# Linear attention on one core: each head pair's output stored by two DMAs of 1 MB in place of one of 2 MB

## The chip, the cores and the metric

The kernel runs on 1 core of a Trainium2 chip. The metric is device microseconds; three runs of the kernel before gave 126.98, 126.93 and 126.97, a median of 126.97.

## What is computed

Linear attention for 8 × 12 heads, 512 positions and 64 features, FP32 in and out:

```python
Q_feat = np.maximum(0, Q) + 1
K_feat = np.maximum(0, K) + 1
KV = np.einsum('bhkd,bhkv->bhdv', K_feat, V)
K_sum = np.sum(K_feat, axis=2)
numerator = np.einsum('bhqd,bhdv->bhqv', Q_feat, KV)
denominator = np.einsum('bhqd,bhd->bhq', Q_feat, K_sum)
return (numerator / (denominator[:, :, :, None] + 1e-10)).astype(np.float32)
```

Three inputs of 12.58 MB are read and one output of 12.58 MB is written.

## The kernel before

The 96 heads are worked on in six steps, numbered s = 0 to 5. The code calls a step a pair: it holds two blocks (n = 0, 1) of eight heads, each block being 128 partitions of 32 rows. So one pair has 1 MB of each input in BF16 (2 MB in FP32) and 2 MB of FP32 output.

All loads but the first half of K go through POOL's DMA queue, which also turns FP32 into BF16 on the way (`load`, line 128). ACT and DVE copy V into a block-diagonal form (L156), DVE makes the features of K and Q (L144, L164), PE sums K features times V (L175), transposes the Q features (L199) and multiplies them by the sums (L216). DVE then takes the reciprocal of the denominators (L232) and multiplies (L233) into the output tile `o_sb`, in eight parts a pair. These are `norms(s, part)`; in the written orders they are called n40 for pair 4, part 0, and so on.

`o_sb` has 128 partitions, eight entries and 2 KB in each entry: 16 KB in a partition. In the output each entry is a block of 256 KB in which every partition owns 2 KB. Part p = 4e + 2i + u writes the entries e + 2u and e + 2u + 4, one half (i) of each: parts 0 to 3 fill the even entries and parts 4 to 7 the odd ones. There are four `o_sb` buffers (`OUT_BUFS`). The first K load borrows one of them at the start, so pair 4 is the first to write into a buffer that has held an output: that of pair 0.

`store(s, ms, engine)` (L135) writes the entries `ms` of pair s. `stores_of(s)` says into how many stores a pair is cut and which parts each needs. Pairs 0 to 3 have one store of all eight entries (2 MB); pair 4 has two, of the even and of the odd entries (1 MB each); pair 5 has one of 1 MB and two of 512 KB. A store is called s20 for pair 2, store 0. Pair 5's are issued by SP on its own queue, the others by POOL.

Each engine's order is written out by hand in `ORDER`, and `trace_all` issues each engine's instructions in exactly that order. POOL's is all loads and then all stores:

```python
POOL="""
    lv2 lk2 lq2 lv3 lq3 lk3 lk4 lv4 lq4 lv5 lk5 lq5 s00 s10 s20 s30 s40 s41
""",
SP="""
    s50 s51 s52
""",
```

(the loads of pairs 0 and 1 come before these). The waits between engines are made from the tiles that instructions read and write.

Of the kernel before, what the change touches and what calls it, by code (L numbers as in the profile page):

```python
# [40 lines left out]
        e40 v500 c43 e41 v511 v512 c42 c50 e50 c51 e51 c53 c52  # L41
    """,
    POOL="""
        lv2 lk2 lq2 lv3 lq3 lk3 lk4 lv4 lq4 lv5 lk5 lq5 s00 s10 s20 s30 s40 s41
    """,
    SP="""
        s50 s51 s52
# [5 lines left out]
def kernel(  # L53
# [210 lines left out]
    last = NPAIR - 1  # L264
    done = set()

    def needs(engine, task):
# [36 lines left out]
        if x == "no":  # L304
            return [("om", s, at[0])] + [("st", s - OUT_BUFS, j) for j in stores_of(s - OUT_BUFS)]
        if x == "st":
            return [("no", s, p) for p in stores_of(s)[at[0]][1]]

    def stores_of(s):

        if s < 0:
            return {}
        if s < last - 1:
            return {0: (slice(0, 8), range(8))}
        halves = {e: (slice(e, 8, 2), range(4 * e, 4 * e + 4)) for e in range(2)}
        if s < last:
            return halves
        return {
            0: halves[0],
            1: (slice(1, 8, 4), (4, 6)),  # L320
            2: (slice(3, 8, 4), (5, 7)),
        }

    def trace(engine, task):
        x, s, *at = task
        if x == "load":
            load(at[0], s)
        elif x == "kf":
            k_features(s, at[0])
        elif x == "vb":  # L330
            copy = nc.vector.tensor_copy if engine == "DVE" else nc.scalar.copy
            v_block(s, at[0], at[1], copy)
        elif x == "qf":
            q_features(s)
        elif x == "kv":
            keys_values(s, *at)
        elif x == "ev":
            weights(s, at[0])
        elif x == "tr":
            transposes(s, at[0])  # L340
        elif x == "tc":
            transposed(s, at[0], nc.vector.tensor_copy if engine == "DVE" else nc.scalar.copy)
        elif x == "om":
            out_matmuls(s, at[0])
        elif x == "no":
            norms(s, at[0])
        elif x == "st":
            store(s, stores_of(s)[at[0]][0], nc.sync if s == last else nc.gpsimd)
# [70 lines left out]
```

## Time and profile before

| | |
|---|---|
| median of 3 runs | 126.97 us |
| profiled execution | 126.98 us |
| its span, first to last instruction | 125.2 us |
| mean granted TensorE clock | 0.924 |
| busy share PE / DVE / ACT / POOL | 65% / 75% / 59% / 18% |
| POOL's DMA queue | 28.84 MB, 94.1% of the DMA engines' span |
| SP's DMA queue | 3.15 MB, 6.8% |
| HBM | 37.75 MB read, 12.58 MB written |
| stores of 2 MB from POOL | 4, median 23.9 us from issue to landing |
| stores of 1 MB from POOL | 2, median 13.5 us |

The span is the time between the first and the last instruction of the profiled execution; what is around it makes up the rest of the 126.98. Lines are marked L and the number in the listing. A DMA has 16 completions, one for each DMA engine, and has landed when its semaphore has all of them; the time from issue to landing holds the time that it waits behind other DMAs of its queue.

### The profile page before, as it was taken

To read this page: it belongs to the slowest core of one execution; us is meant where nothing else is said; L and a number is where in the kernel's file an instruction comes from. 1 tells how busy PE (TensorE), PEld (TensorE's weight loads), DVE (VectorE), ACT (ScalarE), POOL (GpSimd) and SP (SyncE) were. 2 spreads that over 40 slices of the span, in tenths; PEclk is the share of its full clock that TensorE was granted. 3 is DMA by queue.
4 is the path that set the end of the run, shared out by engine and by line. 5 is a ranking of instruction groups with operands and counts; after the bars stand their busy time and mean duration, and the time that the engine had idled before them with its cause. 6 is when DMAs were issued, how large, how long until landed. Compare 5 with 4: busy or idle time off the path is not lost.

```text
span 125.2 us, 2347 instructions
## 1 busy us (share of the span) xinstructions
PE 81.9 (65%) x960; PEld 61.6 (49%) x960; DVE 93.8 (75%) x188; ACT 74.3 (59%) x94; POOL 22.6 (18%) x48
## 2 busy tenths in 40 slices
PE   0000099974989896699439999969997889650000
PEld 0000067853667775477327767656875567430000
DVE  4799962469489796995789799999999796993000
ACT  7538000674856999849990399989999357400000
POOL 6991042000006000060000580002002010200000
PEclk9999999999599999999995999999999999995555
DMA  3999999999999999999999999999999999999992
GB/s 89 339 211 212 217 211 217 211 216 215 215 213 215 222 207 213 215 217 215 215 212 213 221 212 212 212 217 213 216 395 411 417 414 391 390 383 390 386 384 88
DMA packets 8666, 32.12 MB, mean 257 GB/s; under 512 B 464, under 2 KB 464, under 8 KB 8528
## 3 DMA queue, kind: packets, MB, share of 16 engines
q0 software_dynamic: 7440, 28.84, 94.1%
q1 hardware_dynamic: 1216, 3.15, 6.8%
q8 instruction: 7, 0.11, 0.3%
q14 instruction: 3, 0.02, 0.0%
HBM read 37.75 MB, written 12.58 MB: 402 GB/s over the span
## 4 chain that ended last, share of the span: by engine, by line
DMA 54%; DVE 13%; ACT 8%; issue 7%; PE 5%; POOL 3%; POOLq 0%; DVEq 0%
DMA q_raw<-in_Q_dram 34%; DMA out_dram<-o_sb 20%; DVE o_sb L233 7%; ACT v_all L156 5%; DVE qf L164 4%; ACT qt L204 2%; PE kva_ps L175 2%; PE o_ps L216 2%; PE qt_ps L199 1%; DVE recip L232 1%; ACT kva L189 1%; POOL v_raw L128 1%; DVE kf L144 1%; POOL k_raw L128 1%; DVE v_all L156 0%
## 5 line engine op out<-in xcount | busy, mean ns | idle before, releaser
L175 PE MATMUL kva_ps<-v_all,kf 128*128 128x260 bf16 x384 | 54.0, 293 | 21.7 <-DVE v_all L156 17.6
L175 PEld LDWEIGHTS <-kf 128*128 128x128 bf16 x384 | 37.1, 103 | 31.7 <-DVE v_all L156 18.0
L156 ACT COPY v_all<-v_raw 32x2048 bf16<-32x2048 bf16 x19 | 36.0, 1896 | 4.8 <-DVE v_all L258 3.2
L233 DVE TENSOR_TENSOR o_sb<-o_ps,recip 128x512 f32<-128x512 f32 x48 | 33.2, 692 | 2.2 <-DMA out_dram<-o_sb 0.6
L204 ACT COPY qt<-qt_ps 128x1024 bf16<-128x1024 bf16 x24 | 23.8, 1014 | 10.6 <-PE qt_ps L199 10.4
L216 PE MATMUL o_ps<-kva,qt 128*64 128x130 bf16 x384 | 20.3, 229 | 7.8 <-DVE o_sb L233 5.4
L144 DVE TENSOR_SCALAR kf<-k_raw,shift,least 128x2048 bf16<-128x2048 bf16 x22 | 17.1, 819 | 6.9 <-PE kva_ps L175 5.0
L156 DVE COPY v_all<-v_raw 32x2048 bf16<-32x2048 bf16 x29 | 20.2, 697 | 0.8
L216 PEld LDWEIGHTS <-qt 128*64 128x64 bf16 x384 | 12.7, 111 | 16.4 <-DVE o_sb L233 6.8
L189 ACT CAST kva<-kva_ps 64x256 bf16<-64x256 f32 x24 | 8.9, 372 | 17.9 <-PE kva_ps L175 17.5
L199 PE MATMUL qt_ps<-identity,qf 128*128 128x128 bf16 x192 | 14.9, 222 | 1.4 <-DVE qf L164 1.0
L199 PEld LDWEIGHTS <-qf 128*128 128x128 bf16 x192 | 12.1, 99 | 2.9 <-DVE qf L164 1.1
L164 DVE TENSOR_SCALAR qf<-q_raw 128x1024 bf16<-128x1024 bf16 x24 | 8.8, 432 | 5.2 <-DMA q_raw<-in_Q_dram 5.2
L128 POOL DMA_DIRECT2D v_raw<-in_V_dram x7 | 4.8, 687 | 41.0 <-DVE recip L232 18.0
L232 DVE RECIPROCAL recip<-o_ps 128x8 f32<-128x8 f32 x48 | 9.6, 201 | 2.6 <-PE o_ps L216 2.3
L135 POOL DMA_DIRECT2D out_dram<-o_sb x6 | 5.5, 913 | 30.1 <-DVE recip L232 20.6
L128 POOL DMA_DIRECT2D k_raw<-in_K_dram x6 | 4.2, 696 | 12.8 <-DVE kf L144 12.8
L128 POOL DMA_DIRECT2D q_raw<-in_Q_dram x6 | 5.0, 840 | 1.2 <-DVE qf L164 1.2
L258 DVE MEMSET v_all<- 128x2600 f32 x2 | 4.5, 2225 | 1.1 <-issue 1.1
L193 ACT CAST kva<-kva_ps 64x4 bf16<-64x4 f32 x24 | 4.1, 170 | 0.0
L259 ACT COPY v_all<-zero 128x1560 f32<-128x1560 f32 x2 | 2.9, 1488 | 0.0
L144 DVE TENSOR_SCALAR kf<-o_sb,shift,least 128x2048 bf16<-128x2048 f32 x2 | 2.6, 1340 | 0.0
(18 smaller groups left out, 6.6 us busy)
## 6 DMA issues: line engine op xcount, KB each, us to landing
out_dram<-o_sb POOLq DMA_DIRECT2D x4, 2048.0 KB, 23.9
q_raw<-in_Q_dram POOLq DMA_DIRECT2D x6, 1024.0 KB, 21.5
k_raw<-in_K_dram POOLq DMA_DIRECT2D x5, 1024.0 KB, 16.3
v_raw<-in_V_dram POOLq DMA_DIRECT2D x5, 1024.0 KB, 18.4
out_dram<-o_sb POOLq DMA_DIRECT2D x2, 1024.0 KB, 13.5
o_sb<-in_K_dram SPq DMA_DIRECT2D x1, 1024.0 KB, 4.9
v_raw<-in_V_dram POOLq DMA_DIRECT2D x2, 512.0 KB, 8.5
out_dram<-o_sb SPq DMA_DIRECT2D x1, 1024.0 KB, 10.6
```

The source lines that it names most:

```text
L128: nc.gpsimd.dma_start(out=t[:, ns[0] : ns[-1] + 1], in_=drams[x][:, 2 * s + ns[0] : 2 * s + ns[-1] + 1])
L135: engine.dma_start(out=o_dram[:, 8 * s : 8 * s + 8][:, ms], in_=outs[s][:, ms], single_packet=engine is nc.gpsimd,)
L144: nc.vector.tensor_scalar(out=kf[:, :, a], in0=raw["k", s, n], scalar1=shift[:, a : a + 1], scalar2=least[:, a : a + 1], op0=ALU.add, op1= ...
L156: copy(out=v_alls[n][ps, :, b * D : b * D + D], in_=raw["v", s, n][ps])
L164: nc.vector.tensor_scalar(out=qf[:, :, cs, n], in0=rows[:, :, cs], scalar1=1.0, scalar2=1.0, op0=ALU.add, op1=ALU.max,)
L175: nc.tensor.matmul(kva_pss[s, n], lhsT=kfs[s, n][:, c].rearrange("p a d -> p (a d)"), rhs=v_alls[n][:, c], start=(c == 0), stop=(c == ROWS ...
L189: nc.scalar.copy(out=kva[po, a::2, n, 0:D], in_=kva_ps[pi, 0 : 4 * D].rearrange("p (b d) -> p b d", b=4),)
L199: nc.tensor.transpose(qt_ps[:, c, r], qfs[s][:, r, 2 * i + c], identity)
L204: copy(out=qts[s][:, 2 * i : 2 * i + 2], in_=qt_pss.pop((s, i)).rearrange("p c r q -> p c q r"),)
L216: nc.tensor.matmul(o_ps[64 * t : 64 * t + 64, c // 2, (c % 2) * W : (c % 2) * W + W], lhsT=qts[s][:, 4 * i + c, 16 * k : 16 * k + 16], rhs ...
L232: nc.vector.reciprocal(out=recip, in_=cells[:, :, :, :, D:D1])
L233: nc.vector.tensor_tensor(out=outs[s][:, e + 2 * u :: 4, 4 * i : 4 * i + 4].rearrange("p n (b c) d -> p b c n d", b=2), in0=cells[:, :, :, ...
```

## The change

Pairs 0 to 3 are stored like pair 4: one DMA for the even entries, as soon as parts 0 to 3 are done, and one for the odd entries after parts 4 to 7. POOL's order names eight stores for these pairs instead of four. Pairs 4 and 5 are stored as before.

```diff
     POOL="""
-        lv2 lk2 lq2 lv3 lq3 lk3 lk4 lv4 lq4 lv5 lk5 lq5 s00 s10 s20 s30 s40 s41
+        lv2 lk2 lq2 lv3 lq3 lk3 lk4 lv4 lq4 lv5 lk5 lq5 s00 s01 s10 s11 s20 s21 s30 s31 s40 s41
     """,
...
         if s < 0:
             return {}
-        if s < last - 1:
-            return {0: (slice(0, 8), range(8))}
         halves = {e: (slice(e, 8, 2), range(4 * e, 4 * e + 4)) for e in range(2)}
         if s < last:
             return halves
```

## The prediction

> **What bounds the kernel now.** I read the 40 slices first, since the change touches only transfers.
>
> ```profile
> DMA  3999999999999999999999999999999999999992
> GB/s 89 339 211 212 217 211 217 211 216 215 215 213 215 222 207 213 215 217 215 215 212 213 221 212 212 212 217 213 216 395 411 417 414 391 390 383 390 386 384 88
> ```
>
> The 16 DMA engines are full from the second slice to the last but one. The 211 to 222 GB/s of slices 3 to 29 are loads that read FP32 and write BF16, so about 430 GB/s are read; from slice 30 (90.8 us) on there are only stores. No engine row is like this: the page's first part gives DVE, the busiest, 75%. Next I asked where the stores are issued, in the timeline of POOL:
>
> ```profile
> 71.78 0.72 POOL L128 DMA_DIRECT2D q_raw<-in_Q_dram  x1
> 72.50 2.15 POOL L135 DMA_DIRECT2D out_dram<-o_sb  x2
> 85.28 0.89 POOL L135 DMA_DIRECT2D out_dram<-o_sb  x1 [10.63 <-DVE recip L232]
> 95.73 0.91 POOL L135 DMA_DIRECT2D out_dram<-o_sb  x1 [9.56 <-DVE o_sb L233]
> 102.69 0.77 POOL L135 DMA_DIRECT2D out_dram<-o_sb  x1 [6.05 <-DVE recip L232]
> 107.34 0.75 POOL L135 DMA_DIRECT2D out_dram<-o_sb  x1 [3.89 <-DVE recip L232]
> ```
>
> These are, in order, the last load, s00 and s10 together, s20, s30, s40, s41. All stores stand in POOL's order behind all loads. In the trace's DMA records of POOL's queue the last of the 16 completions of each comes at: last load 91.95, s00 97.25, s10 102.30, s20 107.31, s30 113.22, s40 116.12, s41 120.07; then SP's s50 to s52, the last at 123.58. (The waiting engine sees it some 0.5 us later, s00 at 97.75 below.) The queue serves its DMAs in order and each waits for its turn: s20 is issued about 17 us before s10 has landed, s30 11 us before s20 has, s40 10 us before s30 has, s41 9 us before s40 has. So the store stage lasts as long as its bytes take, and not as long as anything that releases them. The last DVE instruction ends at 113.96, 9.6 us before the last landing.
>
> Third, whether anything waits for a store, in the chain of waits (start, length, what) and in DVE's waits:
>
> ```profile
> 72.50 25.25 DMA out_dram<-o_sb
> 97.75 0.03 issue
> 97.78 0.02 DVEq L233
> 97.80 0.04 issue
> 97.84 0.69 DVE o_sb L233
> ```
> ```profile
> DVE o_sb L233 <- DMA out_dram<-o_sb: 0.6, 1, 0.6
> ```
>
> One wait, 0.6 us: n40, the first division of pair 4, writes the o_sb buffer that s00 empties (four buffers, and the first K load has used one of them). The chain shows this as 25 us of DMA, but DVE only waits for the last 0.6 of it.
>
> Last, the store rate in stretches (length, engines, PE clock, DMA share, GB/s at the end):
>
> ```profile
> 92.00:95.00 3.00, 2.33 (x37) 1.66 (x34) 2.93 (x7) 2.94 (x6) 0.00 (x0) 1.00 1.03 423
> 97.00:101.00 4.00, 3.40 (x43) 2.64 (x41) 3.33 (x11) 1.15 (x2) 0.00 (x0) 1.00 1.02 417
> 103.00:107.00 4.00, 3.78 (x64) 2.96 (x64) 2.85 (x8) 3.09 (x8) 0.46 (x1) 1.00 1.03 394
> 107.00:111.00 4.00, 2.21 (x45) 1.36 (x42) 3.73 (x11) 1.01 (x1) 0.75 (x1) 1.00 1.01 385
> 112.50:114.50 2.00, 0.25 (x8) 0.09 (x4) 1.43 (x3) 0.00 (x0) 0.00 (x0) 0.60 1.01 391
> ```
>
> s00 and s10 move at 417 to 423 GB/s, s20 at about 394, s30 at 385, and s40, already a half of 1 MB, at 391. The rate falls while whole stores run, before the first half is in flight.
>
> **The change, part by part.** The sum is made against the profiled execution (126.98 us, span 125.2; 1.8 lie around the span); it is 0.01 above the median of 126.97.
>
> *Bytes and pieces.* Nothing changes: 12.58 MB written, runs of 2 KB at the output in both forms. All POOL store records, those of the halves s40 and s41 too, are 4 KB packets. Cost 0, if the rate stays (see the rivals).
>
> *Four more DMAs in POOL's queue.* Each ends with one completion record on each of the 16 engines. What a DMA costs between others, I take from the loads: 1 MB loads land every 4.895 us, the 512 KB loads at the start every 2.4575. Two small ones take 4.915, so one more DMA costs 0.020 us. For stores the completion record itself takes 9 ns against 22 for loads, which is the low end; the high end would be that half of s10 costs as much as s40, in the first rival. Four times 0.020 = 0.08 us, on the path, since the queue has no gap. I take it, as the loads are the only rows where just the size differs.
>
> The Trainium skill, "DMA: Bandwidth & Descriptors", section "Anatomy of one DMA — SWDGE (gpsimd) path", fits a DMA from GpSimd at about 2.0 us plus its bytes over 436 GB/s; its own account is that most of the 2.0 is waiting for completion. By that formula taken serially, four more DMAs would be an estimated 8 us, a time of 135.0.
>
> *POOL's issue time.* A 1 MB store takes 0.75 to 0.77 us, a 2 MB one 0.89 to 1.18, so s00, s01, s10, s11 take 4 × 0.76 = 3.0 instead of 2.15: 0.9 us more, once, at 72.5. Hidden by the queue's backlog: s00 has its turn only at about 90.6, 15 us after all four are issued. Nothing on POOL is behind them but stores, s20 being ready some microseconds later. Without the backlog it would cost the 0.9.
>
> *Stores issued earlier.* s20 and s30 now wait for four norms instead of eight and go out several microseconds earlier; s21 and s31 go out when the whole ones did. They come to a queue that is busy until 102 and 107, so that brings 0.
>
> *n40's wait.* It needs entries 0 and 4, both in the half with e = 0. If the wait is for that half alone, it ends about 2.5 us before 97.75, and DVE's 0.6 us disappear; if for both, it ends 0.02 to 0.04 later. What is late next is the stores of pairs 4 and 5, at most 0.6 earlier in queues with 9 us of backlog: 0 at the end. Bounds -0.6 to 0, taken 0, because the last landing is 9.6 us behind DVE.
>
> Sum: +0.08 us, 127.05 from the median. A difference of 0.2% is 0.25 us, about what a measurement of this kernel can tell from no change, so this counts as the same.
>
> **Rivals.**
>
> *Slower: halves are written at a lower rate.* A half takes every other entry: its pieces are 4 KB apart in o_sb and 512 KB apart in the output, where those of the whole lie side by side and 256 KB apart. The only half that runs almost alone, s40, lands 2.742 us after s30 (mean over the 16 engines); whole stores take 5.077, 5.015, 5.234 and 5.493. If a half costs 2.742 from the start, eight make 21.94 against 20.82: +1.12 us, 128.1. For it: s00 and s10 are the fastest stores and the only early ones, and no half is seen at 420 GB/s. Against it: s30, whole, is as slow as two times s40, so the fall looks tied to time or place, not to shape. It decides as soon as halves lose over a fifth of this (0.25 us). The early rate is the thing the change could spoil, and there is no row for it; so this stays a large case.
>
> *Faster: the late stores keep the early rate.* I do not know why s20 and s30 are slower than s10 with the same shape. If it is a state that the engines drift into (their completions of one DMA lie 1.4 us apart at the last load, 2.1 at s30), more and shorter DMAs in another order might delay it. At s10's 5.015 per 2 MB, s20 would gain 0.22, s30 0.48, and the 4 MB behind them 0.9: 125.4 with all of it, 126.65 with a quarter. No row shows a half helping.
>
> *Faster by the earlier wait.* The 0.6 us of n40 reach the end: 126.4. Against it are the 9.6 us of backlog. Small.
>
> *Each DMA pays its latency.* If the queue drained before each further DMA, four would cost several microseconds: the first V load of 512 KB lands 6.8 us after its issue by the page's row although its share of the queue is 2.46 us, so 4.3 each, 17 in all, 144. The DMA row of 9s and landings at 4.895 us intervals speak against it. The trace so also disagrees with the skill's formula as a serial cost.
>
> That the change doesn't do what it says I exclude: order and table agree on two stores for each pair up to 4.
>
> **How the numbers follow.** Same, +0.08: 0.43. Slower by the rate: 0.36, and 0.01 for latency. Faster: 0.15 by a kept rate, 0.05 by the wait. The likeliest is the sum, 127.05, whose own range is 126.9 to 127.3. The whole range goes up to the full price of the first rival, 128.1, and down to 126.4; the larger gains of a kept rate and the latency case are left out. Chances: 0.20, 0.43, 0.37.
>
> **What would show it.** Right: landings at mean intervals whose two halves sum to 5.0 to 5.1 in pairs 0 and 1, last completion within 0.25 us of 123.58, DVE's wait for out_dram gone, more POOL busy time and no new wait behind it. The slower rival: 2.7 us for each half from s00 on, and under 400 GB/s in slices 30 to 33. The faster: over 400 in slices 34 to 38. Wrong altogether: a gap in the DMA row, or POOL's later stores waiting for a landing.

## The result, and the profile after

The changed kernel takes 126.67 us (median of 14 runs) against 126.97 (14 runs): a ratio of 0.9974, with a 95% interval of 0.9967 to 0.9981. That is 0.30 us faster, where the prediction had it 0.08 slower, at 127.05 with 126.9 to 127.3 around it. The profiled execution took 126.69 us, its span 124.9.

The 40 slices of the changed kernel:

```profile
DMA  3999999999999999999999999999999999999993
GB/s 87 336 210 214 216 214 216 210 216 215 215 215 210 222 207 218 213 214 218 213 215 215 211 218 211 215 215 213 218 374 419 413 415 392 388 384 382 385 384 146
```

The DMA engines are as full as before, and the fall from between 413 and 419 GB/s to 392 and less is where it was. The same stretches as before (GB/s at the end of a line):

```profile
92.00:95.00 3.00, 3.00 (x39) 2.28 (x37) 2.90 (x6) 2.92 (x7) 0.00 (x0) 1.00 1.03 421
97.00:101.00 4.00, 4.00 (x51) 3.02 (x49) 3.92 (x10) 2.48 (x2) 0.75 (x1) 1.00 1.03 416
103.00:107.00 4.00, 3.78 (x57) 2.79 (x55) 2.85 (x8) 3.15 (x11) 0.75 (x1) 1.00 1.02 393
107.00:111.00 4.00, 2.55 (x48) 1.70 (x48) 3.73 (x10) 1.63 (x2) 0.75 (x1) 1.00 1.02 385
112.50:114.50 2.00, 0.97 (x14) 0.48 (x10) 1.93 (x5) 0.00 (x0) 0.00 (x0) 0.50 1.01 381
```

421, 416, 393, 385 against 423, 417, 394, 385: halves move as whole stores do at the same place. (In the last stretch both kernels write halves, at 381 and 391.) POOL's timeline:

```profile
71.88 0.72 POOL L128 DMA_DIRECT2D q_raw<-in_Q_dram  x1
72.59 3.15 POOL L135 DMA_DIRECT2D out_dram<-o_sb  x4
78.21 0.75 POOL L135 DMA_DIRECT2D out_dram<-o_sb  x1 [2.46 <-DVE recip L232]
86.61 0.75 POOL L135 DMA_DIRECT2D out_dram<-o_sb  x1 [7.65 <-DVE recip L232]
89.97 0.75 POOL L135 DMA_DIRECT2D out_dram<-o_sb  x1 [2.60 <-DVE o_sb L233]
97.15 0.75 POOL L135 DMA_DIRECT2D out_dram<-o_sb  x1 [6.43 <-DVE o_sb L233]
```

s20 and s30 go out 7 to 8 us ahead of s21 and s31, and the four stores of pairs 0 and 1 take 3.15 us of POOL. The output tensor's own view says who waits for a store:

```profile
who waited for it (us, times):
busy tenths in 40 slices 0000000000000000000000072202100202200000
```

Nobody is listed, where before DVE had its 0.6 us.

So far all is as predicted, and none of it makes the kernel faster. The last landing, as the engine that waits for it sees it, is at 124.01 us against 123.92 before: 0.09 us later. The span is nevertheless 0.31 shorter. The time went after the last landing: from there to the end of the span it is 1.28 us before and 0.88 after. These are POOL's last records in the trace (number in order of start, start, length in ns, instruction); of these the profile's page counts only s41 as busy. All but s41 belong to the line that closes the program (L414 in the listing):

```
before                                      changed
66  107.322 14171 DRAIN                     72  108.006 13308 DRAIN
67  107.343   754 DMA (s41)                 73  108.028   752 DMA (s41)
68  124.090    17 wait for all engines      74  124.179    17 wait for all engines
69  124.517    17 release all engines       75  124.261    17 release all engines
70  124.602   141 DRAIN                     76  124.342    88 DRAIN
71  124.772   118 clear semaphores          77  124.459   118 clear semaphores
```

Between the wait and the release of the other engines, POOL stands for 0.427 us before and for 0.082 after; the DRAIN that follows is 0.05 shorter too. Together these 0.40 us, less the 0.09 of the later landing, make the 0.31 of the span. The page has one more difference, in the part on queues. Before:

```profile
q8 instruction: 7, 0.11, 0.3%
q14 instruction: 3, 0.02, 0.0%
```

Changed:

```profile
q8 instruction: 7, 0.11, 0.3%
q14 instruction: 4, 0.03, 0.1%
```

Queue 14 fetches instructions, 8 KB at a time. Three of the records stand at like times in both kernels (43.1, 58.8 to 59.4, 111.8 to 112.6 us). The changed kernel has a fourth at 101.4. The kernel before has its fourth at 125.2, behind the end of its span, as the window from 123.9 to 126 us shows:

```profile
DMA  0000000000000000000000000400000000000000
...
q14 instruction: 1, 0.01, 1.1%
```

### The profile page after: what moved, and what is told of

The parts are those of the page before. It is cut to its first block, busy times and chain, and to the rows that moved or that the text cites. A ratio compares the mean times of both kernels' runs of the same rounds, so it can differ in the third digit from the quotient of the medians.

```text
span 124.9 us, 2353 instructions
## 1 busy us (share of the span) xinstructions
PE 82.9 (66%) x960; PEld 62.1 (50%) x960; DVE 93.8 (75%) x188; ACT 74.2 (59%) x94; POOL 24.8 (20%) x52
## 3 DMA queue, kind: packets, MB, share of 16 engines
q1 hardware_dynamic: 1216, 3.15, 6.9%
## 4 chain that ended last, share of the span: by engine, by line
DMA 39%; DVE 32%; PE 11%; POOL 6%; issue 3%; ACT 1%; POOLq 0%
DMA q_raw<-in_Q_dram 20%; DMA k_raw<-in_K_dram 18%; DVE o_sb L233 14%; PE kva_ps L175 7%; DVE kf L144 6%; DVE v_all L156 5%; DVE recip L232 3%; DVE qf L164 3%; PE o_ps L216 3%; POOL kva L380 2%; POOL v_raw L128 2%; PE qt_ps L199 1%; POOL q_raw L128 1%; POOL k_raw L128 1%; ACT qt L204 1%
## 5 line engine op out<-in xcount | busy, mean ns | idle before, releaser
L216 PE MATMUL o_ps<-kva,qt 128*64 128x130 bf16 x384 | 20.8, 233 | 6.9 <-DVE o_sb L233 4.8
L135 POOL DMA_DIRECT2D out_dram<-o_sb x10 | 7.7, 773 | 28.5 <-DVE recip L232 19.5
```

Source lines behind the costliest of these rows:

```text
L135: engine.dma_start(out=o_dram[:, 8 * s : 8 * s + 8][:, ms], in_=outs[s][:, ms], single_packet=engine is nc.gpsimd,)
L216: nc.tensor.matmul(o_ps[64 * t : 64 * t + 64, c // 2, (c % 2) * W : (c % 2) * W + W], lhsT=qts[s][:, 4 * i + c, 16 * k : 16 * k + 16], rhs ...
```

## The theories

**A**: POOL stands still for about 0.4 us at one place of its instruction stream, where a new block of instructions begins. Four more DMAs and the waits with them (80 POOL records in place of 74) push the end sequence past that place, so that the place falls where POOL waits for a norm anyway. The split itself costs about what the prediction said. **B**: the split helps through the transfers, and the end sequence is a coincidence. **C**: smaller stores are written at a lower rate.

## The experiments

**Whole stores, six more POOL instructions.**

```diff
+    spare = const.tile([P, 16], FP32, name="spare")
...
         for x in "kvq":
             load(x, 1)
+        for i in range(6):
+            nc.gpsimd.memset(spare[:, i : i + 1], 0.0)
```

> The kernel before with its whole 2 MB stores, and six POOL memsets of 1 column into a spare tile behind the loads of pair 1, where POOL is idle. Theory A (the gain is in POOL's end sequence: in the profile of before POOL stands 0.43 us between two semaphore instructions after the last landing, after the change 0.08; POOL's instruction stream is longer after the change, so that an instruction fetch falls into the store stage and not behind the last landing): the gap is 0.08 us, a record of queue 14 stands between 70 and 110 us that before does not have, and the time falls by 0.3 to 0.45 us to about 126.55, below the changed kernel. Rival B (the gain is in the transfers: earlier release, order or rate of the halves): no change, 126.97, and the gap stays at 0.43.

Measured: 126.59 us, ratio 0.9966 (0.9954 to 0.9978). The gap is 0.083 us, the span ends 0.88 us after the last landing, and queue 14 has a record at 101.2 us. The kernel before, with its 2 MB stores and six useless instructions, is as fast as the changed one. Under B it would have stayed at 126.97.

**The changed kernel, ten POOL instructions fewer.**

```diff
-            for k in range(8):
-                nc.gpsimd.memset(t[:, k], 0.0)
+            cuts = (0, 8) if t is kvas[1] else (0, 4, 5, 6, 7, 8)
+            for k0, k1 in zip(cuts, cuts[1:]):
+                nc.gpsimd.memset(t[:, k0:k1], 0.0)
```

> The changed kernel with ten POOL instructions fewer: the 16 memsets that clear the two kva tiles are made 6, with the same area cleared. Theory A: the gap of 0.4 us in POOL's end sequence is back, the time is 126.97 + 0.08 = 127.05 (127.0 to 127.1), slower than before by the cost of four more DMAs. Rival B: 126.67 as in the changed kernel, whatever the gap does.

Measured: 126.99 us, ratio 1.0008 (0.9994 to 1.0021). With the split in place and the stall back, the whole gain is gone. These are POOL's last records:

```
64  124.194    17 wait for all engines
65  124.272    17 release all engines
66  124.353    96 DRAIN
67  124.478   120 clear semaphores
68  124.632    51 DRAIN
69  125.095    17 wait for all engines
70  125.186    17 release all engines
```

The stall was expected between the first wait and release, but it stands five records on: 0.463 us between records 68 and 69, where the other kernels have 0.095. In the kernel before it also stood between 68 and 69. The place is fixed in POOL's stream, and what stands there changes. The window from 123.9 to 126 us has the late fetch again, at 125.8, 0.7 us behind the end of the stall as in the kernel before (125.2):

```profile
DMA  0000000000000000000000000000000000004000
...
q14 instruction: 1, 0.01, 1.2%
```

**Whole stores, one more POOL instruction.** The diff is that of the first experiment with `range(1)`.

> The kernel before with a single POOL memset of 1 column behind the loads of pair 1. Theory A in its sharp form (the stall belongs to the place in POOL's instruction stream between the two end semaphore instructions): with one instruction more the place lies before the wait for all engines, the stall is hidden in it, and the time falls by 0.3 to 0.45 us, as with six. Theory A in a loose form (the place is not that sharp, some instructions' reach): the gap stays and 126.97. Rival B: 126.97.

Measured: 126.65 us, ratio 0.9964 (0.9951 to 0.9978). One memset of one column is enough:

```
67  107.739 13685 DRAIN
68  107.761   752 DMA (s41)
69  124.164    17 wait for all engines
70  124.254    17 release all engines
```

Between records 68 and 69 POOL now waits in any case, first in the DRAIN until 121.42 and then for the other engines until 124.16. The fetch stands at 123.1 us, inside this wait, and the gap from record 69 to 70 is 0.090. This is the sharp form of A.

**Whole stores, ten POOL instructions fewer.** The diff of the second experiment, on the kernel before.

> The kernel before with ten POOL instructions fewer (the same 16 memsets made 6). In the profiles the stall stands behind the same instruction of POOL's stream in two kernels: before has 0.43 us between the 68th and the 69th POOL record, and the changed kernel less ten has 0.46 us between the 68th and the 69th, five records further into the end sequence. Whole stores less ten have only about 64 POOL records. Theory A as a place in the stream: the place is never reached, no stall and no late record of queue 14, and the time falls to 126.5 to 126.65. Theory A as length (a longer stream is better): 126.97 or more.

Measured: 126.83 us, ratio 0.9979 (0.9963 to 0.9994), faster than before but not as fast as expected. POOL has 64 records, no stall in the span, and 0.89 us from the last landing to its end, as A says of the place. But 126.5 to 126.65 did not come: the profiled execution took 126.89 with a span of 124.75, so 2.14 us lie around the span and not 1.77 to 1.80 as in the other eleven profiled kernels. The fetch is at 126.6, among the semaphore events that follow the program in the trace. So the time moved out of the span and did not all go away, and this holds for every run: in the twelve runs 1.94 to 2.19 us lie around the span (spans are on record to 0.1 us), 2.06 in the mean, where the runs of all other kernels have 1.72 to 1.85, and means of 1.76 to 1.78. With 1.78 the median would be an estimated 126.55, inside the 126.5 to 126.65 of A. That the place in the stream is reached behind the span fits this, but the trace keeps no POOL records there that would show it.

**Quarters: 16 stores of 512 KB for pairs 0 to 3.**

```diff
+        if s < last - 1:
+            return {
+                2 * e + u: (slice(e + 2 * u, 8, 4), (4 * e + u, 4 * e + 2 + u))
+                for e in range(2)
+                for u in range(2)
+            }
         if s < last:
             return halves
```

> The changed kernel with pairs 0 to 3 stored by four DMAs of 512 KB each (16 in place of 8). For the cost of one more DMA in a full queue: theory A with 0.020 us a DMA has the last completion 8 x 0.02 = 0.16 us later than in the changed kernel, 126.83. Rival B (finer stores help through release, order or rate): faster than 126.67, by up to the 0.3 that the first split brought. Rival C (smaller stores are written at a lower rate): a store of 512 KB takes over 1.37 us of the queue from pair 0 on, and the time is over 127.5.

Measured: 127.24 us, ratio 1.0015 (0.9995 to 1.0034). The end sequence is the short one (0.88), and the last landing is at 124.68 us, 0.67 after the changed kernel's. None of the three numbers came: B's gain is excluded; A's 0.020 us a DMA is too small; and C in the form expected is out, because the stores of pair 0 take 1.27 us each of the queue (mean over the engines), 5.09 for the pair against 5.00 in halves and 5.08 whole. It is pairs 2 and 3 that grow, to 5.43 and 5.77 from 5.27 and 5.52. So eight further DMAs cost 0.06 to 0.08 each, the lower figure by the queue's time for the four pairs (21.35 us against 20.88, the mean of the three profiles with halves) and the higher by the last landing. That is three to four times the term that I had from the loads.

**Quarters in pairs 0 and 1 alone, and in pairs 2 and 3 alone.** The condition is `s < 2` and `s in (2, 3)`.

> The changed kernel with pairs 0 and 1 alone stored in quarters (four more DMAs, where the stores run at over 410 GB/s). The 16 quarters cost 0.57 us more than halves. If each DMA costs the same, 0.07 us, four give +0.28: 126.95. If the cost is one of the slow late stage, in which engines' completions lie 1.5 to 2.8 us apart, the four cost 0.00 to 0.05 and the time is that of the changed kernel.

> The changed kernel with pairs 2 and 3 alone stored in quarters (four more DMAs, in the stage below 400 GB/s). If each DMA costs the same: +0.28, 126.95. If the cost is one of the slow late stage: +0.45 to 0.6, as with quarters in all four pairs.

Measured: 127.11 us, 1.0003 (0.9982 to 1.0024), and 126.85, 0.9972 (0.9951 to 0.9992); last landings 124.34 and 124.29. By the landings each DMA costs 0.06 to 0.07 us in either stage (against 124.06, the mean of three landings with halves, below). But the late kernel's last load already ended 0.09 us later than with halves. Counted from the last load, the four pairs take 21.15 us with early quarters and 21.01 with late ones, against 20.88: 0.07 us a DMA early and 0.03 late. So it is not the late stage alone that pays; an equal price is not shown either, with one profile each and intervals that overlap. Why a store of 512 KB costs more than the loads' 0.020 stays open.

**Halves and whole stores with the same end sequence, on one chip.** The changed kernel and the whole stores with six memsets, once more.

> The changed kernel again, beside the whole stores with six POOL memsets on the same chip, so that the price of the split is seen with the same end sequence in both. Theory A: 0.08 to 0.1 us slower than those, 0.997 to 0.998 of before. Rival B (the split itself helps a little too): not slower than those.

> Whole stores and six POOL memsets, again. Theory A: 0.996 to 0.997 of before, 0.08 to 0.1 us faster than the changed kernel. Rival B: as the changed kernel or slower.

Measured: 126.66 us, 0.9966 (0.9947 to 0.9985), and 126.69, 0.9962 (0.9944 to 0.9979). The price of the split is too small for this comparison. The landings of all profiles that tell the two apart: whole 123.92, 123.91, 124.11, 123.99, 123.86, mean 123.96; halves 124.01, 124.14, 124.02, mean 124.06. That is +0.10 us, about the size predicted (0.08), but single profiles of one kernel differ by 0.2, and 0.06 of it is there before any store: the last load ends at 91.21 us in the mean with whole stores and at 91.27 with halves (mean over the engines). From there pairs 0 to 3 take 20.86 us whole (20.79 to 20.98) and 20.88 in halves (20.86 to 20.92). The price of the split itself is 0.02 us, which the profiles cannot tell from nothing.

**Pair 4 whole too, with six memsets.** `halves` is returned for no pair but the last one's table, and POOL's order ends `s30 s40`.

> Whole stores with six POOL memsets, and pair 4 stored by one DMA of 2 MB too. Theory A: one DMA fewer, 0 to 0.05 us faster than with two, 126.55 to 126.6, if the one store, issued only when s41 was, still finds the queue full (s30 lands 5 us later). Rival: the store comes too late and opens a gap, over 126.7.

Measured: 126.67 us, 0.9971 (0.9952 to 0.9991), last landing 124.22. No gap, and no gain either. No version tried is faster than the changed kernel by more than the runs can tell.

## Why the prediction was wrong

*What bounds the kernel.* Right. DVE ended 0.7 us later in the changed kernel's profile (114.65 against 113.96) and the last store was issued as much later, with no effect on the last landing, as the prediction's backlog of 9 us says.

*Bytes and pieces, and the first rival.* The rate stayed. The halves of pair 0 land 2.50 and 2.50 us apart (mean over the engines), of pair 1 2.58 and 2.50, of pairs 2 and 3 2.59 to 2.76, as against 2.742 from the start. The eight take 20.87 us where the four took 20.82. The slower rival is out. Two figures of the prediction were slightly off: slice 15 has 207 GB/s, below the 211 that the prediction gives as the lowest, and at s10's rate the 4 MB behind s30 would gain 0.8 us (10.81 us by the mean completions, less twice 5.015) and not 0.9.

*Four more DMAs.* +0.08 predicted. The last landing came 0.09 later in the two profiles and 0.10 in the mean of eight, but more than half of that mean stood before the first store, so the runs show only that the four cost 0.1 us at the most. The 0.020 had been taken from two load intervals, while the intervals of 1 MB loads differ among themselves by 0.1 (4.895 to 4.998 us). The fit of the Trainium skill, "DMA: Bandwidth & Descriptors", section "Anatomy of one DMA — SWDGE (gpsimd) path", read serially gave an estimate of 8 us for four DMAs. The traces disagree with that reading by a factor of 80 or more: halves of 1 MB land 2.50 us apart, about 420 GB/s, which leaves no 2 us of waiting in each.

*POOL's issue time, the earlier stores, n40's wait.* As said: 3.15 us of issue hidden, the wait gone, nothing gained at the end. The faster rivals did not happen: the late rate is 393 and 385 GB/s, as before, and the 0.6 us of n40's wait did not reach the last landing.

*The step that failed* is the first line of the sum: "span 125.2; 1.8 lie around the span". I took all that follows the last landing for a constant, 1.28 us in the span and 1.78 around it, without looking at what it is made of. 0.40 us of it hung on a stall of POOL (0.35 between the wait and the release, 0.05 in the DRAIN behind), and a change that adds instructions to POOL moves it. The prediction said of the added issues only what time they take, and that "Nothing on POOL is behind them but stores"; the end sequence stands behind them. So a term of 0.40 us was put at nothing without a reason. The sum with this term, 0.08 less 0.40, is 126.65; measured 126.67. That it comes so close is partly luck, since the 0.08 is not resolved.

What is shown is that the stall belongs to a place in POOL's stream: one instruction more removes it from the time, ten fewer in the changed kernel bring it back at the same place, and memsets of a spare tile do what the split does. That it has to do with instruction fetches is inferred, from the one 8 KB record of queue 14 that moves with the place (99.5 to 102 us in the eight kernels that pass it amid the stores, 123.1, 125.2, 125.8 and 126.6 in the others) while the other three stay. Where the stall is seen, the record stands 0.7 us after its end, not in it, and in those eight kernels 3.4 to 4.4 us behind POOL's record 69. So this record follows the place, and what exactly POOL waits for there is open. The Trainium skill, "Runtime: NRT & Kernel Launch", section "Instruction fetch mechanics", says that a sequencer fetches the next page while it executes the current one and that crossing a boundary is mostly hidden. If the place is such a boundary, the traces agree where POOL waits for something else, and disagree where the place comes after the last landing: there it costs 0.35 to 0.40 us.

## What to carry to other kernels

A gain of some tenths of a microsecond is not yet a gain of the change: compare the last landing and the time behind it separately, and undo the change with its instruction count kept before believing in it. In this kernel, whose queue never runs dry, it was worth nothing to issue stores earlier or in halves, and quarters cost time. If a kernel ends with a longer gap than its neighbours between two bookkeeping instructions of one engine, one harmless instruction on that engine is a cheap thing to try; here it brought 0.3 us.

## What was not expected of the hardware

One thing is a stall of 0.35 to 0.37 us between records 68 and 69 of POOL's stream, in the two kernels that reach this place after the last landing. The other is that the price of a further store in a full queue is not one number: four more DMAs for halves cost too little to be told from nothing (0.02 us together), while each one for quarters of 512 KB cost 0.03 to 0.08.
